# An encoder layer on one core: the rotary key's projection with high and low weight columns side by side, banks for the last halves, and other due times

## The chip, the core and the metric

The kernel runs on one of the eight cores of a Trainium2 chip. A core has five engines that run side by side and meet only at semaphores: TensorE (PE) for matmuls, with its weight loads (PEld) ahead of them, VectorE (DVE), ScalarE (ACT), GpSimd (POOL), and SyncE (SP), which here only issues DMAs. Every engine takes its own queue in order. PE writes its results to PSUM, eight banks of 128 partitions by 512 fp32 values; DVE and ACT read them from there. The metric is the device time of one execution in microseconds (us).

## What is computed

One layer of an encoder for 512 positions and a model width of 1024. Its reference, cut to what matters here:

```python
h = _rmsnorm(x, norm_mix[i])
proj = h @ w_in[i]
c_q, c_kv, k_pe, u_h = proj[..., :c1], proj[..., c1:c2], proj[..., c2:c3], proj[..., c3:]
q = (_rmsnorm(c_q, q_norm[i]) @ w_uq[i]).reshape(B, S, H, QK_HEAD_DIM)
kv = (_rmsnorm(c_kv, kv_norm[i]) @ w_ukv[i]).reshape(B, S, H, QK_NOPE_DIM + V_HEAD_DIM)
...
k = jnp.concatenate([k_nope, k_pe_h], axis=-1)
...
y_attn = _block_attention(q, k, v).reshape(B, S, MLA_WIDTH)
...
y_hyena = x0 * _bidir_long_conv(x1 * vh, h_fwd, h_bwd, hyena_bias[i])
...
x = x + y_mix @ w_out[i]
...
x = x + (jax.nn.silu(g) * u) @ w_down[i]
e = _rmsnorm(p[i] @ w_ple[i], ple_norm[i])
x = x + jax.nn.sigmoid(x @ w_ple_gate[i]) * e
```

One combined projection yields the query's latent (768 columns), the key and value latent (256), one rotary key of 32 columns (`k_pe`) that all eight heads share, and three inputs of a long convolution (512 each). Attention and convolution are normed, joined and projected; a gated MLP with a short convolution follows, and at the end an embedding (256 wide) that is projected, normed and gated by a sigmoid.

## The kernel before

Activations lie transposed: 128 channels on the partitions, 512 positions along a row. Precision comes from splitting. Each fp32 operand becomes a high part (`hi`, rounded to the matmul's input type, fp32r, by an ACT copy) and a low part (`lo`, the rest, by a DVE subtraction), and `prod3` gives three matmuls for each pair of 128-row tiles: high by high, high by low, low by high. A projection of 1024 inputs to 128 outputs is 8 x 3 = 24 matmuls of 512 columns into one PSUM bank.

PSUM is used by two tags of four banks: `mm` (`mm_ps`) and `ax` (`ax_ps`). A tile takes the bank of the tile four places before it in its tag.

Weights come in a fixed order (`stream`). `wload` loads 1024 columns by SP into one of two raw buffers (`wr`), and splits them into one of three `wh` and three `wl` buffers. From the sixth on, half of the low part is formed by an ACT copy with scale -1 and an accumulating load on POOL's queue. `ahead` keeps three weights recorded ahead of use.

Order is not written by hand. All instructions are first recorded by the class `Plan`. `cost` gives each an estimated duration, `order` gives each a due time and then lists the instructions of every engine: at each step that one which can start first, and among those within 0.02 us the one due first. A due time of a matmul is its place in PE's recorded sequence; any other instruction's is set backwards from the instructions that need its result. Nothing in this says that a bank must be empty for its next tile; a tile only gets a slot when one is free. `STRETCH`, `MARGIN` and the durations in `cost` belong to this planner. The constants at the top (`D_FILT` and the like) delay tasks that are woven into the recorded sequence by `advance`, `ENG` chooses an engine for single operations, `UQ` is the order of the six query projections, `GN` the steps of the attention at which a convolution gate is recorded, and `TAIL` the recorded order of what stands between the query projections and the attention: E and O inverse transforms, V values, G a gate, S scores, P the preparation of the second head, and R, which lets all tasks end and then forms the softmax scale from the sums of the query's squares.

Where the change touches the program:

- After the key and value latents, `in_gemm(2)` projects the rotary key. Its 32 columns are repeated four times, to 128 weight columns, so that every 32 partitions hold a copy. `rms_bcast` forms `R1`, the input norm, spread over partitions by a matmul with ones; DVE multiplies the bank by `R1`, ACT squares it (`pesq`), and `rotate` gives `kpe`.
- Between these, the loads of constants (the rotary table, the identity, selectors, four transform matrices of 512 KB) are recorded. `plan.behind = gate_consts` makes them wait for the POOL addition of the sum of x squared.
- The third and fourth weight of the stream (`w_in[2]` and `w_in[3]`) go through `wload`.
- `embedding`, recorded behind the seventh of eight output projections of the MLP, loads its input `pT`, splits it into `ph` and `pl`, and projects it in 8 x 6 matmuls.
- The last loop gates the embedding for eight tiles: a projection, a sigmoid on ACT out of the bank, a product and a sum on DVE, and the store. For the last tile this is done in two halves of 256 positions, whose matmuls write two halves of one bank. For the planner a matmul touches its whole bank.

Of the kernel before, what the change touches and what calls it, by code (L numbers as in the profile page):

```python
# [25 lines left out]
D_SIN = 2.0  # L26
D_FILT = 13.5
D_TR = 1.0
D_HALF = 8.5
D_RMS = 18.5  # L30
D_LAT = 0.0
D_UU = 13.0
D_UT = 1.0
D_MUL = 3.5
D_SPR = 6.0
D_SQ = 13.0
NTMP = 10
D_LR = 7.0
D_KC = 4.5
D_RC = 2.5  # L40
W0N = 512
# [4 lines left out]
NRH = 15  # L46
D_FT = 11.5
TAIL = 'E0 P E1 R O S0 S1 V0 V1 S2 S3 V2 G0 V3'
ENG = {'pr0': 'G', 'a53': 'V', 'a64': 'V', 'sp3': 'V', 'pr2': 'G', 'sp7': 'G', 'qa2': 'V', 'm5': 'V', 'a51': 'G', 'ah1': 'G', 'hl0': 'V', 'fwo': 'G', 'ah3': 'G', 'qa5': 'V', 'hl2': 'G', 'qa3': 'V', 'm6': 'V', 'm7': 'G', 'm2': 'V', 'qa1': 'V', 'sp5': 'G', 'xt': 'G', 'Uc': 'G', 'sp4': 'G', 'w01': 'V', 'w11': 'V', 'a61': 'G', 'pr3': 'G', 'a67': 'G', 'a63': 'V', 'u4': 'G', 'a65': 'G', 'w10': 'G', 'u3': 'G', 'sp0': 'G', 'eos': 'V', 'vx': 'A', 'vl': 'V', 'vh': 'A', 'va': 'V', 'vf': 'V', 've': 'V', 'vc': 'A', 'sx': 'A', 'sl': 'V', 'sh': 'V', 'sa': 'V', 'sf': 'V', 'se': 'V', 'sc': 'A', 'qa4': 'G', 'sp6': 'V', 'm4': 'V', 'rot2': 'G', 'cv5': 'V', 'm1': 'G', 'a62': 'V', 'rot1': 'G'}
ATT = {'pr', 'a', 'ah', 'hl', 'xt'}  # L50
PRI = {'rows': 500, 'val': 20, 'kt': 60, 'rms': -120, 'cols': 400, 'H': 0, 'gate': 150, 'uT': -120, 'io': -20, 'sq': 20, 'turn': 0, 'so': -300, 'fold': -120, 't8': 0, 'gsq': -50, 'ie': 400}
QACT = 0
UQ = [5, 2, 4, 3, 0, 1]
D_KS = 6.0
D_KR = 5.0
D_TAIL = 16.5
RFILL = 4
# [3 lines left out]
FILLS = (16, 24, 32)  # L61
GN = (4, 6, 7, 9)
CPRI = 50
EPS = 1e-6
MARGIN = 0.1
AIM = 0.0
STRETCH = {'V': 1.05, 'S': 1.05, 'G': 1.05, 'PE': 1.0, 'SP': 1.0}
NH = 8
# [154 lines left out]
class Plan:  # L223
# [50 lines left out]
    def cost(self, op):  # L274
# [11 lines left out]
        if op.eng == "PE":  # L286
            if op.fn == "transpose":
                op.dur = 0.11 if a[1].shape[0] > 8 else 0.07
            elif a[1].dtype == F32:
                op.dur = max(0.222, 0.855 * n / T) if n > 8 else 0.222  # L290
            else:
                op.dur = (n + 32) / 2400.0
            op.lat = 0.25
        elif op.eng == "V":
            if op.fn == "reduce_max":
                op.dur = 0.6
            elif op.fn in ("tensor_tensor", "stream_shuffle"):
                op.dur = 0.07 + n / 960.0
            elif op.fn == "reciprocal":
                op.dur = 0.1  # L300
            elif op.fn == "tensor_scalar" and not any(isinstance(v, View) for v in a[2:]) and not a[1].tile.tag.pool.psum:
                op.dur = 0.08 + n / 1900.0
            else:
                op.dur = 0.12 + n / 960.0
            op.lat = 0.22
            ins = [v for v in list(a[1:]) + list(kw.values()) if isinstance(v, View) and v.shape[1] * len(v.shape) > 16]
            op.port = n > 64 and len(ins) > 1 and not any(v.tile.tag.pool.psum for v in ins)
        elif op.eng == "S":
            op.dur = 0.09 + n / 1190.0
            if isinstance(kw.get("scale"), View) or isinstance(kw.get("bias"), View):  # L310
                op.dur += 0.06
            if kw.get("accum_out") is not None:
                op.dur += 0.15
            op.lat = 0.24
            op.table = TABLES.get(a[2])
        elif op.eng == "G":
            op.dur = 0.05 + (n / 780.0 if op.fn == "tensor_scalar" else n / 410.0)
            op.port = n > 64 and op.fn != "memset"
        else:
            op.dur = 0.1  # L320

    def order(self):
        clock = 5.5
        for op in self.ops:
            if op.eng == "PE":
                op.due = clock
                clock += op.dur
            else:
                op.due = None
            for p in op.preds:  # L330
                p.succs.append(op)
        for op in reversed(self.ops):
            need = clock + 50.0 if op.due is None else op.due
# [113 lines left out]
def tile_encoder_block(  # L447
# [50 lines left out]
    def wload(src, n, cut):  # L498
# [23 lines left out]
    def ahead(i):  # L522
        while len(ready) < min(i, len(stream)):
            with nullcontext():
                ready.append(wload(*stream[len(ready)]))

# [337 lines left out]
    plan.behind = None  # L864
    ckv = [xpool.tile([P, T], F32, tag="x", name="x") for _ in range(2)]
    for i in range(2):
        V.tensor_tensor(ckv[i], kv_ps[i], R1, op=ALU.mult)
    pe = tmp()
    V.tensor_tensor(pe, pe_ps, R1, op=ALU.mult)
    S.activation(pesq, pe, AF.Square)  # L870
    S.activation(pe, pe, AF.Copy, scale=pcol("gk_r"))
# [558 lines left out]

    def embedding():
# [3 lines left out]
        split(ph, pl, ptr)  # L1435
        pp = [(ph[:, i * T : (i + 1) * T], pl[:, i * T : (i + 1) * T]) for i in range(2)]
        for m in range(8):
# [16 lines left out]
    for m in range(8):  # L1454
        ps = mm_ps()
        o = 0
        for ci, nk in enumerate((8, 8, 6)):
            w = next_w()
            mms(ps, prod3(wtiles(w, nk), hid[o : o + nk]), start=ci == 0, stop=ci == 2)
            o += nk  # L1460
# [4 lines left out]
        if m == 6:  # L1465
            embedding()

    Re = const.tile([P, T], F32, tag="R1", name="Re")
    for m in range(8):
        w = next_w()  # L1470
        ps = mm_ps()
        halves = ((0, T),) if m < 7 else ((0, 256), (256, T))
        for a, b in halves:
            mms(ps[:, a:b], prod3(wtiles(w, 8), [tuple(v[:, a:b] for v in k) for k in x2]))
        if m == 0:
            rms_bcast(Re, acc7, 1024, tt4, "e")
        V.scalar_tensor_tensor(ev[m], ev[m], pcol("g_ple", m), Re, op0=ALU.mult, op1=ALU.mult)
        t = tt4()
        for a, b in halves:
            S.activation(t[:, a:b], ps[:, a:b], AF.Sigmoid)  # L1480
# [74 lines left out]
def _layout(d):  # L1555
# [99 lines left out]
```

## Time and profile before

| | us |
|---|---|
| median of 3 runs | 739.68 (739.25 to 739.82) |
| profiled execution | 739.88 |
| its span, first to last instruction | 738.1 |
| idle of PE before its first matmul | 5.68 |

The span is the part of the time in which instructions run. In the profile every instruction stands at line 441, the planner's call that issues it, so groups are told apart by tile names: `mm` and `ax` are the banks, `wh`, `wl` and `wr` the weights, `a`, `g`, `x` and `t` activations. A matmul's row gives its own time with its way through the array, about 0.39 us; in an unbroken sequence the starts lie closer together than that, and the distance of the starts is what a matmul costs. "[3.54 <-ACT t L441]" behind a row says that the engine was idle for 3.54 us before it and which instruction ended the wait. An "x2" joins two neighbours in one row.

### The profile page before, as it was taken

The page shows a single profiled execution, that of the slowest core. Times are in us where ns is not written, and L with a number is a line of the kernel's source. Part 1 is how long each engine was busy: PE and PEld are TensorE (multiplying, and loading weights), DVE is VectorE, ACT ScalarE, POOL GpSimd, SP SyncE. Part 2 cuts the span into 40 slices and gives each one's busy share as a digit, 9 for nine tenths or more (in the row PEclk, how much of TensorE's full clock was granted, in tenths as well). Part 3 has the DMA queues.
Part 4 walks back from the last instruction along what each step waited for, and adds up shares of the span by engine and source line. Part 5 has one row for each costly group of instructions (what it writes and reads, how often), then busy time and mean ns, then how long its engine had stood idle before and what let it go on. Part 6 is the DMA issues. An engine that isn't in the chain of part 4 may idle for free.

```text
span 738.1 us, 9053 instructions
## 1 busy us (share of the span) xinstructions
PE 718.2 (97%) x3254; PEld 580.8 (79%) x3254; DVE 509.6 (69%) x768; ACT 370.8 (50%) x579; POOL 177.1 (24%) x158
## 2 busy tenths in 40 slices
PE   6999999998989999999999999999999999999997
PEld 4777888875577788878888888888888888878886
DVE  6698999998689986878676676676765223242383
ACT  7564455387779985545443443434433222235331
POOL 1211101011047872422223223223322000004000
PEclk9999999999999999999999999999999999999999
DMA  7776573555352412523323223233232332333321
GB/s 246 241 187 161 124 185 86 114 122 131 75 175 59 107 44 57 133 96 89 111 87 104 97 87 113 86 97 103 86 107 81 98 114 83 96 117 106 110 104 71
DMA packets 30111, 82.83 MB, mean 112 GB/s; under 512 B 3914, under 2 KB 5258, under 8 KB 30067
## 3 DMA queue, kind: packets, MB, share of 16 engines
q1 hardware_dynamic: 24674, 72.01, 31.3%
q0 software_dynamic: 5392, 10.25, 7.4%
q8 instruction: 25, 0.41, 0.2%
q14 instruction: 20, 0.16, 0.1%
HBM read 77.00 MB, written 2.10 MB: 107 GB/s over the span
## 4 chain that ended last, share of the span: by engine, by line
PE 55%; DVE 1%; issue 0%; ACT 0%; DVEq 0%
PE mm L441 38%; PE ax L441 18%; DVE a L441 0%; DVE pl L441 0%; DVE t L441 0%; ACT t L441 0%; DVEq L1650 0%; DVE x L441 0%
## 5 line engine op out<-in xcount | busy, mean ns | idle before, releaser
L441 PE MATMUL mm<-a,wh 128*128 128x512 f32 (+1 forms) x928 | 310.4, 390 | 6.9 <-ACT wh L441 6.8
L441 ACT ACTIVATE wh<-wr 128x1024 fp32r<-128x1024 f32 (+2 forms) x117 | 119.1, 1020 | 256.3 <-PE mm L441 192.5
L441 PEld LDWEIGHTS mm<-a,wh 128*128 128x128 f32 x928 | 173.3, 189 | 45.2 <-ACT wh L441 7.6
L441 PE MATMUL mm<-a,wl 128*128 128x512 f32 (+1 forms) x464 | 171.9, 391 | 0.0
L441 DVE TENSOR_TENSOR wl<-wr,wh 128x1024 fp32r<-128x1024 f32 (+3 forms) x117 | 121.3, 1040 | 68.9 <-ACT wh L441 68.7
L441 PE MATMUL ax<-a,wh 128*128 128x512 f32 x384 | 147.1, 389 | 0.0
L441 PEld LDWEIGHTS mm<-a,wl 128*128 128x128 f32 x464 | 87.4, 189 | 19.1 <-DVE t L441 0.8
L441 DVE SCALAR_TENSOR_TENSOR f<-f,par,f 128x511 f32<-128x511 f32 x88 | 85.9, 980 | 2.7 <-ACT f L441 1.2
L441 PEld LDWEIGHTS ax<-a,wh 128*128 128x128 f32 x384 | 72.0, 188 | 14.9
L441 PE MATMUL mm<-g,wh 128*128 128x512 f32 x232 | 80.1, 397 | 3.5 <-ACT t L441 3.5
L441 PE MATMUL ax<-a,wl 128*128 128x512 f32 x192 | 74.7, 389 | 0.0
L441 PE MATMUL mm<-h,wh 128*128 128x512 f32 x192 | 65.9, 389 | 0.0
L441 POOL TENSOR_TENSOR f<-f,f 128x512 f32<-128x512 f32 x22 | 29.3, 1331 | 143.4 <-DVE f L441 125.2
L441 PEld LDWEIGHTS mm<-g,wh 128*128 128x128 f32 x232 | 43.9, 190 | 14.7 <-ACT t L441 4.0
L441 DVE TENSOR_TENSOR f<-mm,R 128x512 f32<-128x512 f32 x22 | 15.2, 691 | 46.4 <-PE mm L441 46.3
L441 POOL TENSOR_TENSOR acc<-acc,t 128x512 f32<-128x512 f32 x13 | 18.8, 1448 | 113.8 <-ACT t L441 103.1
L441 PE MATMUL mm<-g,wl 128*128 128x512 f32 x116 | 45.2, 395 | 0.0
L441 PEld LDWEIGHTS ax<-a,wl 128*128 128x128 f32 x192 | 36.0, 188 | 7.5
L441 PEld LDWEIGHTS mm<-h,wh 128*128 128x128 f32 x192 | 36.0, 188 | 7.5
L441 POOL DMA_DIRECT2D wl<-in_w_in_dram x16 | 13.9, 871 | 102.4 <-DVE wl L441 40.0
L441 ACT ACTIVATE f<-f,par 128x512 f32<-128x512 f32 x44 | 35.3, 806 | 5.2 <-DVE f L441 5.2
L441 PE MATMUL mm<-h,wl 128*128 128x512 f32 x96 | 37.4, 389 | 0.0
(242 smaller groups left out, 1007.5 us busy)
## 6 DMA issues: line engine op xcount, KB each, us to landing
wr<-in_w_up_dram SPq DMA_DIRECT2D x44, 512.0 KB, 3.5
wr<-in_w_in_dram SPq DMA_DIRECT2D x19, 512.0 KB, 3.9
wr<-in_w_down_dram SPq DMA_DIRECT2D x16, 512.0 KB, 3.5
x<-in_xT_dram SPq DMA_DIRECT2D x16, 256.0 KB, 4.4
wl<-in_w_in_dram POOLq DMA_DIRECT2D x16, 256.0 KB, 5.2
wr<-in_w_out_dram SPq DMA_DIRECT2D x8, 512.0 KB, 4.2
wr<-in_w_gate_dram SPq DMA_DIRECT2D x8, 512.0 KB, 3.5
wr<-in_w_down_dram SPq DMA_DIRECT2D x8, 384.0 KB, 3.1
```

What stands on the lines that cost most here:

```text
L441: getattr(self.handles[op.eng], op.fn)(*[real(v) for v in op.args], **{k: real(v) for k, v in op.kw.items()})
```

## The change

The rotary key's weight now has 64 distinct columns in place of 128: for each of the eight 128-row tiles, 32 columns twice. `wload_pe` loads them as 512 columns and writes the high parts into columns 0 to 63 and the low parts into columns 64 to 127 of one tile. One matmul with all 128 columns against the high part of x gives high by high on partitions 0 to 63 and low by high on 64 to 127; a second one with the 64 high columns against the low part of x adds into partitions 0 to 63. ACT copies the two halves of the bank crosswise into a temporary tile, and DVE adds bank and copy, so that each of the four groups of 32 partitions holds the whole sum. Its product with `R1` then comes from there.

`wload_halves` loads and splits `w_in[3]` in two halves by temporary tiles. The loads of constants are recorded behind the whole rotary key and wait for `pesq`. `embedding_input` loads and splits `pT` when the seventh output projection is begun. In the last loop each half of the last tile gets a bank of its own. In `order`, an instruction that touches a PSUM tile is also due before the first instruction of the tile that takes its bank, if that is recorded later. Further, `cost` has other durations for small DVE instructions, PSUM readers and ACT, and the delays, `UQ`, `GN`, `TAIL`, `ENG`, `STRETCH` and `MARGIN` have other values.

```diff
-D_FILT = 13.5
-D_TR = 1.0
-D_HALF = 8.5
-D_RMS = 18.5
+D_FILT = 13.0
+D_TR = 2.0
+D_HALF = 7.0
+D_RMS = 30.5
...
-D_SPR = 6.0
-D_SQ = 13.0
+D_SPR = 3.5
+D_SQ = 2.0
...
-TAIL = 'E0 P E1 R O S0 S1 V0 V1 S2 S3 V2 G0 V3'
+TAIL = 'R E0 E1 O P V0 S0 S1 V1 S2 G0 V2 S3 V3'
...
-UQ = [5, 2, 4, 3, 0, 1]
-D_KS = 6.0
-D_KR = 5.0
-D_TAIL = 16.5
+UQ = [5, 0, 4, 1, 2, 3]
+D_KS = 2.0
+D_KR = 7.0
+D_TAIL = 14.5
...
-GN = (4, 6, 7, 9)
+GN = [4, 6, 5, 11]
...
-MARGIN = 0.1
+MARGIN = 0.05
 AIM = 0.0
-STRETCH = {'V': 1.05, 'S': 1.05, 'G': 1.05, 'PE': 1.0, 'SP': 1.0}
+STRETCH = {'V': 1.05, 'S': 1.03, 'G': 1.05, 'PE': 1.0, 'SP': 1.0}
...
+            elif n <= 32:
+                op.dur = 0.13 if op.fn == "tensor_scalar" else 0.22
...
+            elif op.fn == "tensor_scalar":
+                op.dur = 0.3 + n / 960.0
...
-            op.dur = 0.09 + n / 1190.0
+            op.dur = max(0.14, (0.05 if a[1].tile.tag.pool.psum else 0.09) + n / 1170.0)
...
+        for pool in self.pools:
+            for tag in pool.tags.values():
+                for k, tile in enumerate(tag.tiles):
+                    tile.heir = tag.tiles[k + tag.bufs] if k + tag.bufs < len(tag.tiles) else None
         for op in reversed(self.ops):
             need = clock + 50.0 if op.due is None else op.due
             for s in op.succs:
                 need = min(need, s.due - op.dur - op.lat - AIM - (2.0 + op.byte / 2.0e5 if op.byte else 0.0))
+            for tile in {x[0] for x in op.acc}:
+                heir = tile.heir if tile.tag.pool.psum else None
+                if heir is not None and heir.first.i > op.i:
+                    need = min(need, heir.first.due - op.dur - op.lat)
             op.due = need
...
+    def wload_pe():
+        raw = tmp()
+        SP.dma_start(raw, w_in[2][:, 0:T])
+        both = wpool.tile([P, 1024], F32R, tag="wh", name="wh", bufs=3)
+        r3 = raw.rearrange("p (k c) -> p k c", k=8)
+        w3 = both.rearrange("p (k c) -> p k c", k=8)
+        S.activation(w3[:, :, 0:64], r3, AF.Copy)
+        V.tensor_tensor(w3[:, :, 64:P], r3, f32(w3[:, :, 0:64]), op=ALU.subtract)
+        return both, None
+
+    def wload_halves(src):
+        hi = wpool.tile([P, 1024], F32R, tag="wh", name="wh", bufs=3)
+        lo = wpool.tile([P, 1024], F32R, tag="wl", name="wl", bufs=3)
+        for a in (0, T):
+            raw = tmp()
+            SP.dma_start(raw, src[:, a : a + T])
+            split(hi[:, a : a + T], lo[:, a : a + T], raw)
+        return hi, lo
...
-    pe_ps = in_gemm(2)
+    pe_ps = mm_ps()
+    pe_w = next_w()[0]
+    for k in range(8):
+        both, high = (pe_ps, pe_w[:, k * P : (k + 1) * P], xs[k][0]), (pe_ps[0:64, :], pe_w[:, k * P : k * P + 64], xs[k][1])
+        for part in (both, high) if k == 0 else (high, both):
+            PE.matmul(*part, start=k == 0 and part is both, stop=k == 7 and part is both)
+        advance(T_IN / 12)
     rms_bcast(R1, accx, 1024, tmp, "x")
-    plan.behind = gate_consts
+    ckv = [xpool.tile([P, T], F32, tag="x", name="x") for _ in range(2)]
+    for i in range(2):
+        V.tensor_tensor(ckv[i], kv_ps[i], R1, op=ALU.mult)
+    pe = tmp()
+    other = tmp()
+    S.activation(other[0:64, :], pe_ps[64:P, :], AF.Copy)
+    S.activation(other[64:P, :], pe_ps[0:64, :], AF.Copy)
+    V.tensor_tensor(other, pe_ps, other, op=ALU.add)
+    V.tensor_tensor(pe, other, R1, op=ALU.mult)
+    late = S.activation(pesq, pe, AF.Square)
+    plan.behind = late
...
+        if m == 6:
+            pin = embedding_input()
...
-        ps = mm_ps()
         halves = ((0, T),) if m < 7 else ((0, 256), (256, T))
-        for a, b in halves:
+        t = tt4()
+        for i, (a, b) in enumerate(halves):
+            ps = mm_ps()
             mms(ps[:, a:b], prod3(wtiles(w, 8), [tuple(v[:, a:b] for v in k) for k in x2]))
...
```

More of the change, by code (lines that the diff above doesn't have):

```diff
@@ L26 @@
 D_SIN = 2.0
-D_FILT = 13.5
-D_TR = 1.0
-D_HALF = 8.5
-D_RMS = 18.5
+D_FILT = 13.0
+D_TR = 2.0
+D_HALF = 7.0
+D_RMS = 30.5
 D_LAT = 0.0
 D_UU = 13.0
-D_UT = 1.0
-D_MUL = 3.5
-D_SPR = 6.0
-D_SQ = 13.0
+D_UT = 0.5
+D_MUL = 3.0
+D_SPR = 3.5
+D_SQ = 2.0
 NTMP = 10
-D_LR = 7.0
-D_KC = 4.5
-D_RC = 2.5
+D_LR = 12.0
+D_KC = 6.0
+D_RC = 4.0
 W0N = 512
@@ L46 @@
 NRH = 15
-D_FT = 11.5
-TAIL = 'E0 P E1 R O S0 S1 V0 V1 S2 S3 V2 G0 V3'
-ENG = {'pr0': 'G', 'a53': 'V', 'a64': 'V', 'sp3': 'V', 'pr2': 'G', 'sp7': 'G', 'qa2': 'V', 'm5': 'V', 'a51': 'G', 'ah1': 'G', 'hl0': 'V', 'fwo': 'G', 'ah3': 'G', 'qa5': 'V', 'hl2': 'G', 'qa3': 'V', 'm6': 'V', 'm7': 'G', 'm2': 'V', 'qa1': 'V', 'sp5': 'G', 'xt': 'G', 'Uc': 'G', 'sp4': 'G', 'w01': 'V', 'w11': 'V', 'a61': 'G', 'pr3': 'G', 'a67': 'G', 'a63': 'V', 'u4': 'G', 'a65': 'G', 'w10': 'G', 'u3': 'G', 'sp0': 'G', 'eos': 'V', 'vx': 'A', 'vl': 'V', 'vh': 'A', 'va': 'V', 'vf': 'V', 've': 'V', 'vc': 'A', 'sx': 'A', 'sl': 'V', 'sh': 'V', 'sa': 'V', 'sf': 'V', 'se': 'V', 'sc': 'A', 'qa4': 'G', 'sp6': 'V', 'm4': 'V', 'rot2': 'G', 'cv5': 'V', 'm1': 'G', 'a62': 'V', 'rot1': 'G'}
+D_FT = 8.0
+TAIL = 'R E0 E1 O P V0 S0 S1 V1 S2 G0 V2 S3 V3'
+ENG = {'pr0': 'G', 'a53': 'V', 'a64': 'V', 'sp3': 'V', 'pr2': 'G', 'sp7': 'G', 'qa2': 'V', 'm5': 'V', 'a51': 'G', 'ah1': 'G', 'hl0': 'V', 'fwo': 'G', 'ah3': 'G', 'qa5': 'V', 'hl2': 'G', 'qa3': 'V', 'm6': 'V', 'm7': 'G', 'm2': 'V', 'qa1': 'V', 'sp5': 'G', 'xt': 'G', 'Uc': 'G', 'sp4': 'G', 'w01': 'V', 'w11': 'V', 'a61': 'G', 'pr3': 'G', 'a67': 'G', 'a63': 'V', 'u4': 'G', 'a65': 'G', 'w10': 'G', 'u3': 'G', 'sp0': 'G', 'eos': 'V', 'vx': 'V', 'vl': 'V', 'vh': 'A', 'va': 'A', 'vf': 'V', 've': 'A', 'vc': 'A', 'sx': 'A', 'sl': 'A', 'sh': 'A', 'sa': 'V', 'sf': 'V', 'se': 'A', 'sc': 'A', 'qa4': 'G', 'sp6': 'V', 'm4': 'V', 'rot2': 'G', 'cv5': 'V', 'm1': 'G', 'a62': 'V', 'rot1': 'G', 'ah0': 'V'}
 ATT = {'pr', 'a', 'ah', 'hl', 'xt'}
@@ L300, in cost @@
                 op.dur = 0.1
-            elif op.fn == "tensor_scalar" and not any(isinstance(v, View) for v in a[2:]) and not a[1].tile.tag.pool.psum:
+            elif n <= 32:
+                op.dur = 0.13 if op.fn == "tensor_scalar" else 0.22
+            elif op.fn == "tensor_scalar" and not a[1].tile.tag.pool.psum:
                 op.dur = 0.08 + n / 1900.0
+            elif op.fn == "tensor_scalar":
+                op.dur = 0.3 + n / 960.0
             else:
@@ L316, in cost @@
         elif op.eng == "G":
-            op.dur = 0.05 + (n / 780.0 if op.fn == "tensor_scalar" else n / 410.0)
+            op.dur = 0.05 + (n / 780.0 if op.fn == "tensor_scalar" else n / 420.0)
             op.port = n > 64 and op.fn != "memset"
@@ L524, in ahead @@
             with nullcontext():
-                ready.append(wload(*stream[len(ready)]))
+                i = len(ready)
+                ready.append(wload_pe() if i == 2 else wload_halves(w_in[3]) if i == 3 else wload(*stream[i]))
     def next_w():
@@ L864, in tile_encoder_block @@
     plan.behind = None
[L865 to L870, printed above, removed]
     S.activation(pe, pe, AF.Copy, scale=pcol("gk_r"))
@@ L1429, in tile_encoder_block, with embedding_input @@
     ev = []
-    def embedding():
+    def embedding_input():
         ptr = wpool.tile([P, 1024], F32, tag="wr", name="wr", bufs=2)
@@ L1435, in embedding @@
         split(ph, pl, ptr)
+        return ph, pl
+    def embedding(ph, pl):
         pp = [(ph[:, i * T : (i + 1) * T], pl[:, i * T : (i + 1) * T]) for i in range(2)]
@@ L1465, in tile_encoder_block @@
         if m == 6:
-            embedding()
+            embedding(*pin)
     Re = const.tile([P, T], F32, tag="R1", name="Re")
@@ L1470, in tile_encoder_block @@
         w = next_w()
-        ps = mm_ps()
         halves = ((0, T),) if m < 7 else ((0, 256), (256, T))
-        for a, b in halves:
+        t = tt4()
+        for i, (a, b) in enumerate(halves):
+            ps = mm_ps()
             mms(ps[:, a:b], prod3(wtiles(w, 8), [tuple(v[:, a:b] for v in k) for k in x2]))
[L1475 to L1479, printed above, removed]
+            if m == 0:
+                rms_bcast(Re, acc7, 1024, tt4, "e")
+            if i == 0:
+                V.scalar_tensor_tensor(ev[m], ev[m], pcol("g_ple", m), Re, op0=ALU.mult, op1=ALU.mult)
             S.activation(t[:, a:b], ps[:, a:b], AF.Sigmoid)
@@ L1588, in _layout @@
     out["w_in"] = mk(a["w_in"][0], 8, in_sel)
+    out["w_in"][2, :, 0:512] = mk(a["w_in"][0], 8, [np.tile(1024 + r(32), 2)])[0]
+    out["w_in"][2, :, 512:] = 0.0
     out["w_uq"] = mk(a["w_uq"][0], 6, uq_sel)
```

## The prediction

> **What bounds the kernel now.** First the head of the page and its busy times.
>
> ```profile
> span 738.1 us, 9053 instructions
> ...
> PE 718.2 (97%) x3254; PEld 580.8 (79%) x3254; DVE 509.6 (69%) x768; ACT 370.8 (50%) x579; POOL 177.1 (24%) x158
> ```
>
> TensorE (PE) is busy for 97% of the span, so the time is its work plus its holes. Where the holes are is told by the table of windows (columns: window, length, busy of PE, weight load, DVE, ACT, POOL with counts, granted clock, DMA share, GB/s), whose rows come from several such tables:
>
> ```profile
> 20.00:174.35 154.35, 153.97 (x668) 121.90 (x667) 140.07 (x234) 85.23 (x129) 22.09 (x28) 1.00 0.59 150
> ...
> 60.00:160.00 100.00, 100.00 (x450) 82.63 (x449) 94.48 (x160) 52.79 (x81) 12.95 (x15) 1.00 0.52 126
> 160.00:180.00 20.00, 16.46 (x68) 11.17 (x66) 18.09 (x32) 14.71 (x26) 3.45 (x4) 0.98 0.64 151
> ...
> 200.00:220.00 20.00, 18.14 (x95) 14.04 (x94) 16.23 (x43) 15.01 (x37) 6.13 (x7) 1.00 0.61 177
> 220.00:240.00 20.00, 19.21 (x119) 15.93 (x118) 19.55 (x52) 19.79 (x42) 15.69 (x18) 1.00 0.27 65
> ...
> 178.28:182.32 4.04, 4.04 (x13) 2.85 (x14) 3.23 (x7) 3.98 (x10) 0.00 (x1) 0.62 0.78 191
> ```
>
> PE is full from 20 on but for 0.38 us, until a hole near 175 with a slow clock behind it; more holes lie in the attention from 200 on, where DVE and ACT are nearly full too. The waits of PE give the causes (total, times, longest):
>
> ```profile
> PE mm L441 <- ACT wh L441: 6.8, 2, 5.7
> PE mm L441 <- ACT t L441: 3.5, 1, 3.5
> PE ax L441 <- DVE ptl L441: 1.5, 1, 1.5
> PE ax L441 <- DVE pl L441: 1.0, 1, 1.0
> PE ax L441 <- DVE st L441: 0.8, 2, 0.4
> PE mm L441 <- ACT pth L441: 0.5, 2, 0.3
> PE ax L441 <- ACT pr L441: 0.5, 1, 0.5
> ```
>
> Of the 6.8 us, 5.7 are the first inputs' way, and the change leaves these loads as they are. The other rows are what it can reach. Where there is no hole, a matmul costs its start-to-start step; the chain that ended last has one long unbroken piece of 512-column matmuls:
>
> ```profile
> 564.28 97.06 PE mm L441 x428
> ```
>
> 97.06 / 428 = 0.227 us each.
>
> **The change part by part.** *Rotary key, 24 matmuls to 16.* Eight fewer: 8 x 0.227 = 1.82 us. They stand on the path, because PE is full there. Eight of the sixteen have 64 weight columns instead of 128. No row shows that shape; the nearest has 8 columns:
>
> ```profile
> 194.93 0.62 PE L441 MATMUL ax<-t,sel 128*8 128x512 f32 x2
> ...
> 178.64 0.57 ACT L441 ACTIVATE t<-ax 8x512 f32<-8x512 f32 x1
> ...
> L441 DVE TENSOR_TENSOR t<-mm,R x21: 669/681/692, 29.3 to 300.0; 128x512 f32<-128x512 f32 x21
> ```
>
> Two take 0.62 with the last one's own 0.40 in it, a step of 0.22 to 0.23: few columns are no cheaper and no dearer. Bounds for the eight: 0 and 1.8; I take no saving. The merge of the two halves adds two ACT copies from PSUM (0.57 each by the 8-row one) and one DVE addition (0.68 by the bank readers). Set against them, this weight is split at half width, so one saves about the other. What waits for the result is the rotary part of the keys, which meets the other parts only after the query projections, and PE's bank comes free without the norm that its reader waits for today. I cost it at nothing; if the cover were gone, it would be 2 x 0.57 + 0.68 = 1.8, all of the gain. The two half loads of the next weight go into temporary tiles and split in halves, at two more fixed parts of an instruction, hidden likewise.
>
> *PSUM readers due with their bank.* The new rule makes an instruction that reads a bank due before the first write of the tile that takes the bank next. The case for it is the second hole:
>
> ```profile
> 174.35 0.39 PE L441 MATMUL mm<-g,wl 128*128 128x512 f32 x1
> 178.28 0.73 PE L441 MATMUL mm<-g,wh 128*128 128x512 f32 x2 [3.54 <-ACT t L441]
> ...
> 172.34 0.62 ACT L441 ACTIVATE t<-accy 128x512 fp32r<-128x512 f32 x1
> 174.55 1.06 ACT L441 ACTIVATE wh<-wr 128x1024 fp32r<-128x1024 f32 x1 [1.59 <-PE mm L441]
> ...
> 177.55 0.67 ACT L441 ACTIVATE t<-mm,par 128x512 f32<-128x512 f32 x1
> ```
>
> PE waits for the bank of a finished query projection. Its copy (t<-mm,par) stands in ACT's queue behind a weight split that waits 1.59 us for a buffer, and behind four more instructions. Ahead of the split, in those idle 1.59 us, the copy would have been done before PE asks at 174.58. So the whole hole goes: 178.28 - 174.35 - 0.227 = 3.70 us. What is late next is the weight split, by one copy of 0.67; it is of the value weights, which come into use behind the query projections. Behind the hole the clock falls: in the window from 178.28 its mean is 0.62, so 0.38 x 4.04 = 1.5 us are lost, which go with the hole.
>
> The same rule acts on the attention's banks:
>
> ```profile
> 215.30 0.75 DVE L441 SCALAR_TENSOR_TENSOR a<-x,par,a 128x512 fp32r<-128x512 f32 x1 [0.64 <-ACT a L441]
> ...
> 216.30 0.68 DVE L441 TENSOR_TENSOR ptl<-ax,pth 128x512 fp32r<-128x512 f32 x1
> ...
> 217.13 0.63 PE L441 MATMUL ax<-ident,a 128*128 128x128 f32 x4 [1.51 <-DVE ptl L441]
> ```
>
> DVE does a low half for a later GEMM before the split that empties the bank. Bounds: 0 (DVE is 19.55 of 20 busy just behind, so a hole filled here may open there) and 1.5. I take the middle, 0.75.
>
> *Embedding's input sooner.*
>
> ```profile
> 656.00 0.33 SPq L441 DMA_DIRECT2D wr<-in_pT_dram  x1
> ...
> 661.36 0.69 DVE L441 TENSOR_TENSOR x<-x,mm 128x512 f32<-128x512 f32 x1 [1.94 <-PE mm L441]
> ...
> 661.96 1.22 DVE L441 TENSOR_TENSOR pl<-wr,ph 128x1024 fp32r<-128x1024 f32 x1
> ...
> 663.24 0.50 PE L441 MATMUL ax<-pl,wh 128*128 128x512 f32 x1 [1.01 <-DVE pl L441]
> ```
>
> The low half is split only behind the bank's reader at 661.36. Recorded one projection earlier (66 matmuls, 15 us), load and split are done long before. The 1.0 us goes; the weights behind it on SP are later by one 0.33 issue and one buffer, under a stage in which DVE and ACT are mostly idle.
>
> *Banks for the last halves.*
>
> ```profile
> 733.38 0.66 ACT L441 ACTIVATE t<-mm 128x256 f32<-128x256 f32 x2 [1.32 <-PE mm L441]
> 733.80 0.76 DVE L441 TENSOR_TENSOR t<-t,f 128x256 f32<-128x256 f32 x2 [0.29 <-ACT t L441]
> 734.48 0.75 DVE L441 TENSOR_TENSOR t<-t,x 128x256 f32<-128x256 f32 x2
> ```
>
> Both halves' gates, products and sums follow the last matmul, to 735.23. With a bank of its own the first half is out earlier, and one of each remains: the second product starts 0.76 / 2 behind 733.80 and takes about 0.4, to 734.56. Gain 0.7 us.
>
> *Constants behind the key's square.* Two DMA issues on SP and six with a memset on POOL move from a wait for a POOL addition to one for ACT's square near 30. The first weights gain what these transfers took from them, which can't be more than the 0.38 us that PE lacks in 20 to 174; behind the moved ones stand weight loads on both queues, and the price of that, up to 2 us, is worked out in the rivals. I take 0, since the weights are recorded three ahead.
>
> *New costs, delays and lists.* They add and remove no instruction, and shift the order by fractions of a microsecond in the stages that PE fills. Bounds: the other waits of the attention above gone, or a bare chain; both are rivals, and I take 0.
>
> Sum: 1.8 + 3.7 + 1.5 + 0.75 + 1.0 + 0.7 = 9.45. The profiled execution took 739.88 (span 738.1, 1.8 around it), 0.2 over the median of 739.68; from the median, **730.2 us**.
>
> **The rivals.** *The hole only moves (0.18).* ACT is busy for 14.7 of 20 us in 160 to 180, and DVE for 94% over 60 to 160; if the readers come late because these engines are late, and not because of their order, some or all of the hole returns. For it: the rows above show ACT without a pause from 174.55 on. Against: it paused 1.59 just before. Half the hole back, without the clock (the 1.51-us hole at 217 left the clock at 1.00 in its row): 730.2 + 1.85 = 732; all of it back with the clock: 735.4, and without the attention's gain 736.2.
>
> *The clock's share is not regular (0.05).* The profiled execution lost 1.5 to the clock; if the others did not, the gain is that much smaller: 731.7. The three runs of before span 0.57 us (739.25 to 739.82), which speaks for one loss in all of them. [...]
>
> *The attention gives more (0.12).* All 1.5 of the hole at 217, and up to the 0.8, 0.5 and 0.5 of the last three waits above: 730.2 - 0.75 - 1.8 = 727.7.
>
> *The constants get in the way (0.06).* Their loads now wait for an ACT instruction near 30, and the accumulating weight loads queue behind them on POOL:
>
> ```profile
> 21.52 0.58 POOL L441 DMA_DIRECT2D dft<-in_c_dft_dram  x1
> 35.94 0.90 POOL L441 DMA_DIRECT2D wl<-in_w_in_dram  x1 [13.84 <-DVE t L441]
> ...
> 29.99 0.63 ACT L441 ACTIVATE qr<-t 128x512 f32<-128x512 f32 x1 [2.65 <-DVE t L441]
> ...
> L441 PE MATMUL ax<-g,qs x24: 389/389/389, 75.2 to 114.9; 128*128 128x512 f32 x24
> ```
>
> Six issues at 0.58 to 0.90 are 3.5 to 5.4 us from 30 on, to 33.5 to 35.4, where the first accumulating load stands today. A constant itself is not needed before 75. If that load slips by 2, PE waits up to 2: 732.
>
> *Slower: the scale chain stands in PE's queue (0.05).* The list of the tail now begins with R, which ends the tasks and forms the softmax scale; before it stood behind both even inverses and prep. PE takes its queue in order. If the turns of this chain come ahead of the inverses and values that fill PE today, PE waits at each hop.
>
> ```profile
> 185.77 1.02 PE L441 MATMUL ax<-accx,ones 128*8 128x512 f32 x2
> ...
> 203.91 0.19 DVE L441 SCALAR_TENSOR_TENSOR sT<-sT,qs 128x32 f32<-128x32 f32 x1
> ```
>
> The chain runs for 18.3 us, all filled today. Bare by more than the 9.45 gained, it ends slower; bare for 15, 745. Against it: the order is made from ready times, so a fill goes first as long as these are about right.
>
> **Chances.** Forecast (728.5 to 732) 0.52; the hole moves 0.18, the clock 0.05, the attention 0.12, the constants 0.06, slower 0.05; 0.02 for gains that cancel. Faster by over 0.2% (1.5 us, about what a measurement here can tell) holds nearly all but the last two: 0.90; same 0.04, slower 0.06, the slower rival and a little of the hole's with more than one hole. Range 727 to 736.5: it takes in the forecast and the rivals but the slower one, and leaves out some 0.12.
>
> **What would show it.** Eight matmuls fewer into the key's bank, and PE's count at 3246; no PE wait on ACT t near 170 and the granted clock 1.00 from 160 to 200; no wait on pl; one sigmoid behind the last matmul; PE's waits in 200 to 280 no longer. It is wrong if a hole of over 1 us stands at another place of 160 to 280, or if PE waits near 40.

## The result, and the profile after

The changed kernel takes 727.53 us (median of 4 runs, 726.46 to 728.12) where the kernel before took 739.55 (739.25 to 739.82) on the same chip: a ratio of 0.9828, 95% interval 0.9811 to 0.9845, so 12 us less by the medians and 12.7 by the ratio. The forecast was 730.2. Scaled to the 739.68 from which it started, the result is 726.96, just under the lower end of the range (727). The direction was right, the reasons only in part, and the gain was a quarter to a third larger than the 9.45 us of the forecast. One execution among all that follow was slow (808.34 us, of the rotary key alone with a tile elsewhere), and its ratio leaves it out.

The head and the busy times of the page after:

```profile
span 726.3 us, 9038 instructions
...
PE 713.0 (98%) x3246; PEld 578.6 (80%) x3246; DVE 504.5 (69%) x766; ACT 377.9 (52%) x588; POOL 178.9 (25%) x158
```

The eight matmuls are gone (3254 to 3246). The waits of PE after (total, times, longest):

```profile
PE mm L453 <- ACT wh L453: 6.8, 2, 6.3
PE mm L453 <- DVE a L453: 0.9, 1, 0.9
PE ax L453 <- DVE st L453: 0.7, 1, 0.7
PE ax L453 <- ACT pr L453: 0.4, 1, 0.4
PE mm L453 <- ACT pth L453: 0.2, 1, 0.2
```

The waits on `t`, `ptl` and `pl` of before have left the list, and there is a new one, on `a`. By stage, from the first matmul on `ckh` (the high part of the key and value latent, with which the up-projection begins) to the first score and from there to the last turn (columns as before), first of the kernel before, then of the changed one:

```profile
148.92:206.70 57.78, 54.24 (x222) 36.74 (x221) 47.22 (x89) 43.19 (x83) 7.03 (x9) 0.97 0.51 115
206.70:277.72 71.02, 67.70 (x406) 55.71 (x405) 65.51 (x165) 64.69 (x139) 49.92 (x53) 1.00 0.32 91
```

```profile
147.02:196.40 49.38, 49.38 (x216) 34.76 (x215) 44.33 (x85) 40.70 (x79) 6.92 (x8) 1.00 0.52 115
196.40:267.71 71.31, 69.61 (x415) 57.36 (x414) 67.58 (x168) 66.20 (x144) 50.05 (x55) 1.00 0.37 102
```

The first stage is 8.4 us shorter: PE has no hole in it and the clock never falls. ACT's order there after:

```profile
168.44 0.67 ACT L453 ACTIVATE t<-mm,par 128x512 f32<-128x512 f32 x1
170.38 0.85 ACT L453 ACTIVATE wh<-wr 128x768 fp32r<-128x768 f32 x1 [1.27 <-PE mm L453]
171.13 0.58 ACT L453 ACTIVATE accy<-mm 128x512 f32<-128x512 f32 x1
...
180.09 1.05 ACT L453 ACTIVATE wh<-wr 128x1024 fp32r<-128x1024 f32 x1
```

The copy that empties the first query projection's bank (168.44) now stands ahead of the split of the value weights (the one with 1024 columns, 180.09), as the prediction wanted, and even ahead of the last query weight's (170.38). Whether the bank rule put it there is what the experiments asked.

To compare stages in which the number of matmuls differs, the tables below give what PE lost in a stretch: its length less the steps of its matmuls (0.227 us for 512 columns and less in proportion, 0.11 to 0.12 for 256, about 0.47 for the full-precision ones with `ones` and `x`, 0.085 for a transposition, 0.32 for a selector, all read from unbroken pieces). A wrong step would shift both columns alike, so the differences are what counts. A turn is the transposition of one block of 128 by 512 attention weights, four matmuls with the identity; there are 32. Of the profiled executions, in us:

| stretch | before | after |
|---|---|---|
| first matmul to the first `ident,pq` matmul of the mixer (some 93) | 5.5 | 5.0 |
| first `ckh` matmul to first score | 8.7 | 1.6 |
| first score to ninth turn | 5.5 | 4.0 |
| ninth to last turn | 6.7 | 6.5 |
| last turn to the MLP's norm | 0.5 | 1.2 |
| first `ph` matmul to the embedding's norm | 1.3 | 0.0 |

The span fell by 11.8: 1.8 for eight matmuls, 0.5 in the first stretch, 7.0 behind `ckh`, 1.6 in the attention, 1.3 at the embedding, 0.8 behind the last matmul; 0.6 were given back by a later first matmul (6.30, before 5.68; in the 18 profiles of this document it starts anywhere between 5.55 and 7.14) and 0.7 in the output projection.

### The profile page after: what moved, and what is told of

It is laid out like the page before. It is cut to its first block, busy times and chain, and to the rows that moved or that the text cites. A ratio compares the mean times of both kernels' runs of the same rounds, so it can differ in the third digit from the quotient of the medians.

```text
span 726.3 us, 9038 instructions
## 1 busy us (share of the span) xinstructions
PE 713.0 (98%) x3246; PEld 578.6 (80%) x3246; DVE 504.5 (69%) x766; ACT 377.9 (52%) x588; POOL 178.9 (25%) x158
## 4 chain that ended last, share of the span: by engine, by line
PE 90%; ACT 4%; DVE 3%; issue 1%; DMA 1%; POOL 1%; SPq 0%; ACTq 0%; POOLq 0%; DVEq 0%
PE mm L453 64%; PE ax L453 26%; ACT pr L453 1%; DVE st L453 1%; DMA wr<-in_w_in_dram 1%; ACT pth L453 1%; DVE ptl L453 1%; ACT a L453 0%; DVE t L453 0%; ACT t L453 0%; POOL pr L453 0%; ACT ks L453 0%; DVE a L453 0%; SPq L453 0%; DVE x L453 0%
## 5 line engine op out<-in xcount | busy, mean ns | idle before, releaser
L453 PE MATMUL mm<-a,wh 128*128 128x512 f32 (+2 forms) x928 | 310.2, 391 | 7.7 <-ACT wh L453 6.8
L453 ACT ACTIVATE wh<-wr 128x1024 fp32r<-128x1024 f32 (+2 forms) x115 | 116.6, 1016 | 188.1 <-PE mm L453 178.6
L453 PEld LDWEIGHTS mm<-a,wh 128*128 128x128 f32 (+1 forms) x928 | 173.8, 189 | 45.2 <-ACT wh L453 7.5
L453 PE MATMUL mm<-a,wl 128*128 128x512 f32 (+1 forms) x456 | 168.1, 391 | 0.0
L453 DVE TENSOR_TENSOR wl<-wr,wh 128x1024 fp32r<-128x1024 f32 (+3 forms) x115 | 119.4, 1041 | 66.9 <-ACT wh L453 66.8
L453 PE MATMUL mm<-g,wh 128*128 128x512 f32 x232 | 78.0, 392 | 0.0
L453 ACT ACTIVATE f<-f 128x512 f32<-128x512 f32 x22 | 13.9, 632 | 56.1 <-DVE f L453 56.1
```

Of the source, the lines that this page charges most:

```text
L453: getattr(self.handles[op.eng], op.fn)(*[real(v) for v in op.args], **{k: real(v) for k, v in op.kw.items()})
```

## Experiments: one part alone

**The bank rule alone**, the kernel before with

```diff
+            for tile in {x[0] for x in op.acc}:
+                heir = tile.heir if tile.tag.pool.psum else None
+                if heir is not None and heir.first.i > op.i:
+                    need = min(need, heir.first.due - op.dur - op.lat)
```

> The kernel before with nothing but the bank rule in the planner. If the hole behind 174.35 is a fault of order (theory), PE's wait on ACT t is gone or under 0.5 us, the granted clock is 1.00 from 160 to 200, and the time is 733.5 to 735 (739.6 less 5.2, or less 5.2 and up to 0.75 in the attention). If the new delays, lists and costs are what closes it (rival), PE still waits over 2 us for an ACT copy in 165 to 185, and the time is within 2 us of 739.6.

Measured: 740.74, ratio 1.0016 (1.0007 to 1.0025). The waits of PE:

```profile
PE mm L449 <- DVE a L449: 2.2, 1, 2.2
PE mm L449 <- ACT t L449: 1.5, 1, 1.5
```

The hole behind the up-projection is halved (3.5 to 1.5) and its slow clock gone, but a hole of 2.2 opens in the output projection at 295 us, with 3.41 us of half clock behind it (mean granted clock 0.997 over the span). The rule alone brings nothing. ACT's queue shows why half the hole stays:

```profile
173.87 1.06 ACT L449 ACTIVATE wh<-wr 128x1024 fp32r<-128x1024 f32 x1 [1.59 <-PE mm L449]
174.83 0.67 ACT L449 ACTIVATE t<-mm,par 128x512 f32<-128x512 f32 x1
```

The rule took the copy past the four other instructions, but not past the split, which waits the same 1.59 us as before.

**The new delays, lists, engine choices and durations alone** (called the new figures below):

```diff
...
-D_SQ = 13.0
+D_SQ = 2.0
...
-UQ = [5, 2, 4, 3, 0, 1]
...
-D_TAIL = 16.5
+UQ = [5, 0, 4, 1, 2, 3]
...
+D_TAIL = 14.5
...
```

> The kernel before with only the new delays, lists, engine choices and planner durations. Theory (moves only): within 3 us of 739.6, the wait on ACT t still above 2 us. Rival: the hole closes by these alone, 733 to 736, wait on ACT t under 0.5 us.

Measured: 741.31, ratio 1.0015 (0.9999 to 1.0031). The same hole is nearly closed (`ACT t` 0.6), without the rule: the copy (177.91) now stands ahead of the split of the value weights (178.65); others open at 49 to 67 us and at 209 (`DVE x` 2.5).

**The rotary key alone** (`wload_pe`, `wload_halves`, 16 matmuls, merge; the constants at their old place):

> The kernel before with only the rotary key in 16 matmuls (its weight's load and split, the half loads of the next weight, the crosswise merge); constants still behind the sum of x squared. Theory: eight matmuls at 0.227 us are gone from a full PE, the key stage ends 1.8 us sooner and, with the hole unchanged, the time is 737.2 to 738.2. Rival (DVE and ACT take it back, or the hole grows by it): 739 to 740, the wait on ACT t longer by 1.5 to 1.8 us.

Measured: 751.46, ratio 1.0160 (1.0145 to 1.0175), 12 us slower where 2 less were due. PE's waits show one of 8.7 us on `pth`, which the prediction had not named. It is followed up below.

**The embedding's input and the halves' banks alone:**

```diff
+        if m == 6:
+            pin = embedding_input()
...
-        ps = mm_ps()
...
-        for a, b in halves:
...
+        for i, (a, b) in enumerate(halves):
+            ps = mm_ps()
...
```

> The kernel before with only the embedding's input one projection earlier and a bank for each last half. Theory: the wait on pl (1.0 us by the waits, about 1.2 from start to start) is gone and the stretch from the last matmul to the end is 0.7 us shorter: 737.5 to 738. Rival (the weights behind the earlier load are late, or a store of the first half delays the second): the one or the other is under 0.3, time 738.5 to 739.6.

Measured: 737.81, ratio 0.9978 (0.9969 to 0.9987). These two do what they say, 1.6 us.

## Experiments: all but one part

**Without the bank rule:**

> The changed kernel without the bank rule, all else kept. Theory: a wait of PE on ACT t or on another reader of a bank comes back in 150 to 200 with 2 to 5 us in all, and the attention's waits grow by 0.5 to 1.5; time 730 to 734. Rival (delays, lists and costs do it): no wait over 1 us there, time within 1.5 us of 727.5.

Measured: 741.35, ratio 1.0027 (1.0014 to 1.0040). The stretch behind `ckh` loses 1.5 us, as little as with the rule, but PE waits 8.2 us for `pth` at 207.

**With the old figures** (delays, lists, engine choices and durations):

> The changed kernel with the delays, lists, engine choices and planner durations of before; the rotary key, the bank rule, the embedding and the halves as changed. Of the 12 us gained, 9.45 were worked out from these four. Theory: the rest of 2 to 3 us is the new delays and lists, so the time is 729 to 731. Rival (the four were undersized and the lists do nothing): within 1 us of 727.5. Other rival (structure and lists only work together): over 733, with a hole of over 2 us in 30 to 280.

Measured: 752.44, ratio 1.0178 (1.0163 to 1.0193). Again 8.1 us on `pth`, and holes of 1.5 to 2.2 at 52, 178 and 309 us.

**With the constants at their old place:**

```diff
-    plan.behind = late
+    plan.behind = gate_consts
```

> The changed kernel with the loads of constants waiting again for the sum of x squared. Theory (the move costs and brings nothing): within 1 us of 727.5, the first 100 us as in the changed kernel to 0.7 us. Rival: the early constants take bandwidth from the first weights and PE waits 1 to 2 us more on weights in the first 40 us, time 728.5 to 729.5.

Measured: 727.04, ratio 0.9841 (0.9819 to 0.9863), not to be told from the changed kernel. Moving the constants costs and brings nothing that shows.

**With the rotary key in 24 matmuls** (and, as before, the constants early):

> The changed kernel with the rotary key in 24 matmuls, loaded, merged and gated as before. Theory: slower by 1.8 us, 729.3 (728.8 to 730.3). Rival (the delays are set for 16 matmuls, so the order falls apart): over 731, with a new wait of PE of over 1 us in 20 to 280.

Measured: 733.49, ratio 0.9916 (0.9895 to 0.9936), 6 us more than with 16, not 1.8: it has new waits on `wl` (0.9) at 50 us and `a` (1.4) at 209, and 3.4 us of half clock.

So the parts don't add. Before one can say what a part is worth, the 8-us hole of three of these runs has to go.

## Experiments: where a tile lies

In the run with the rotary key alone, SyncE's DMA issues around the attention's start, SyncE's waits there, ScalarE's row and PE's wait:

```profile
198.41 1.16 SPq L441 DMA_DIRECT2D qr<-g  x2
210.17 1.10 SPq L441 DMA_DIRECT2D kr<-x  x2
...
214.71 1.12 SPq L441 DMA_DIRECT2D kr<-x  x2
```

```profile
SPq L441 <- PE ax L441: 10.9, 1, 10.9
```

```profile
221.54 0.63 ACT L441 ACTIVATE ks<-kr 96x512 fp32r<-96x512 f32 x1 [8.27 <-DMA kr<-x]
```

```profile
PE mm L441 <- ACT pth L441: 8.7, 1, 8.7
```

Read backwards: PE waits for `pth`, an ACT copy; ACT stands 8.27 us before `ks<-kr`, which waits for the raw key's load; SyncE issued that load at 214.71, late behind another `kr` (210.17, of head 2), for which it had waited 10.9 us on PE. That `kr` copies a tile that PE does not write. But it lies in memory that the closed pool `ft` held before, and a tile's place is given out in the order in which tiles are first touched. From the built programs (bytes per partition):

```
                     kr of head 2      over                 last read by
before               216992 to 219040  uu0, pq0             transforms, early
changed              216992 to 219040  uu2                  transforms, early
rotary alone         216992 to 219040  ckl1                 value matmuls
without bank rule    216992 to 219040  ckl1                 value matmuls
old delays           216992 to 219040  ckl1                 value matmuls
```

`ckl1` is a low part of the key and value latent; the last matmul that reads it starts at 209.74 us in the run above, and SyncE goes on at 210.17 (the row of the wait names a neighbour of that matmul on PE). The three kernels with the hole are those where `kr` lies over it. A test that changes the place and leaves the order of every engine's instructions as it is (the two built programs differ in addresses and in waits alone):

```diff
-                raw = pool.tile([P, T], F32, tag=f"{nm}r", name=f"{nm}r")[0:96, :]
+                raw = (at if nm + pool.name == "qap" else pool).tile([P, T], F32, tag=f"{nm}r", name=f"{nm}r")[0:96, :]
```

> Same order of instructions on every engine as the run with the rotary key alone (751.46 us). Only the place in SBUF differs: the raw query of the heads with a pool of their own lies in the pool ahead, so that the raw key of head 2 (kr) moves up by 2 KB and lies over the input's tile uu1, last read early, and no longer over ckl1, last read by the value matmuls. Theory (placement): SyncE's wait on PE before kr (10.9 us in that run) and the 8.7 us hole in the attention's start are gone, and with them the 10.6 us that the stretch from the first score to the eighth turn lost over the kernel before: 736 to 741 us, near the kernel before less the 1.8 us of the eight matmuls (737.7). Rival (order): the list's order of the work causes the hole, and the time stays at 751 +- 1.

Measured: 741.92, ratio 1.0023 (1.0009 to 1.0036), 9.5 us less than the same order at the old place, and a little over the expected band (the kernel before took 740.03 beside it). SyncE's issues and PE's first waits:

```profile
198.67 1.16 SPq L441 DMA_DIRECT2D qr<-g  x2
199.87 1.23 SPq L441 DMA_DIRECT2D kr<-x  x2
...
204.54 1.12 SPq L441 DMA_DIRECT2D kr<-x  x2
```

```profile
PE mm L441 <- ACT wh L441: 6.4, 1, 6.4
PE mm L441 <- ACT t L441: 3.5, 1, 3.5
PE ax L441 <- DVE st L441: 2.8, 5, 1.3
```

`kr` follows `qr` at once, and the wait for `pth` is down to 0.3. The stretch from the first score to the ninth turn loses 5.45, to the hundredth what the kernel before loses.

The same edit in the other two kernels:

> The changed kernel without the bank rule (741.35 us), with the same order of instructions on every engine and the raw key of head 2 at another place. Theory (placement): the hole before the value side's first weighing (8.2 us, and 10 us of half clock behind it) is gone, 12.4 us less in the stretch from the first score to the eighth turn: 728 to 731 us; the bank rule would then be worth 1 to 3 us of the change and not the whole. Rival (order, so the bank rule itself): 741 +- 1.

Measured: 732.84, ratio 0.9889 (0.9866 to 0.9913): 8.5 us less, but 2 above the expected band.

> The changed kernel with the old delays and cost model (752.44 us), same order of instructions, raw key of head 2 at another place. Theory (placement): 10.6 us less, 739 to 743 us; the holes at 51, 178 and 309 us stay, since they have nothing to do with the place. Rival (order): 752 +- 1.

Measured: 741.36, ratio 1.0022 (1.0006 to 1.0038): 11 us less, within the band.

And the other way round: the changed kernel with the key put over a late tile (the edit above, and `ab` of "k" moved to `at` likewise), again with each engine's order as it was.

> The changed kernel (727.5 us), same order of instructions on every engine; the raw query and the split key of the heads' second pool lie in the pool ahead, so that the raw key of head 2 lies over ckl0, last read by the value matmuls at about 203 us, and not over uu2. Theory (placement): SyncE waits some 9 us for PE before this transfer (issued at 193.4 us without the wait), the next key's transfer (197.1 us) goes to about 206.5 us, ScalarE stands before its ks for some 6 us, and matmuls wait for pth: 731 to 739 us. Rival (order): 727.5 +- 1.

Measured: 737.22, ratio 0.9952 (0.9936 to 0.9968): 9.7 us slower than the changed kernel, by place alone. SyncE's issues in the changed kernel, then here, and ScalarE and PE here:

```profile
192.14 1.18 SPq L453 DMA_DIRECT2D qr<-g  x2
193.36 1.23 SPq L453 DMA_DIRECT2D kr<-x  x2
...
197.07 1.12 SPq L453 DMA_DIRECT2D kr<-x  x2
```

```profile
192.37 1.17 SPq L453 DMA_DIRECT2D qr<-g  x2
203.83 1.11 SPq L453 DMA_DIRECT2D kr<-x  x2
...
207.43 1.11 SPq L453 DMA_DIRECT2D kr<-x  x2
```

```profile
214.15 0.63 ACT L453 ACTIVATE ks<-kr 96x512 fp32r<-96x512 f32 x1 [7.43 <-DMA kr<-x]
```

```profile
PE mm L453 <- ACT pth L453: 7.8, 1, 7.8
```

Same chain, same size. By the ratios to the kernel before, which ran beside each, place is worth 9 to 12 us in all four pairs. The kernel before and the changed one both lie on the good side, so it is no part of the 12 us.

## Experiments: what the rest is made of

With the place mended the parts can be compared (ratio to the kernel before; a single part without the others, a pair of parts and all three with the embedding and the halves, which are worth 0.9978; "delays" stands for all new figures). In none of these runs does PE wait for `pth` longer than 0.4 us at a time, so none has the hole of the last section:

| | ratio |
|---|---|
| rule / delays / rotary key alone | 1.0016 / 1.0015 / 1.0023 |
| rule and rotary key | 1.0022 |
| rule and delays | 0.9916 |
| delays and rotary key | 0.9889 |
| all three | 0.9828 |

The new figures of the planner are in every row that gains. Taken out of the changed kernel they cost 14 us (1.0022 less 0.9828), the rotary key 6.5, the rule 4.5; each of the three put alone into the kernel before brings nothing. By stretch, what PE lost with the place mended:

| stretch | before | after | no rule | old figures |
|---|---|---|---|---|
| start | 5.5 | 5.0 | 4.8 | 7.9 |
| `ckh` to first score | 8.7 | 1.6 | 1.5 | 5.2 |
| first score to ninth turn | 5.5 | 4.0 | 7.7 | 4.8 |
| ninth to last turn | 6.7 | 6.5 | 10.3 | 8.3 |
| last turn to the MLP's norm | 0.5 | 1.2 | 0.1 | 4.7 |

So the rule earns nothing behind the up-projection once the figures are new; in these executions (6.1 us apart, where the ratios say 4.5) it earns 7.4 us in the attention and costs 1.1 in the output projection. Against the kernel before, though, the attention gains 1.6 only: without the rule the changed kernel loses 5.8 more there than the kernel before (the new figures alone lose 3.2), and the rule takes these back. Without it PE's largest waits in the attention are

```profile
PE ax L445 <- ACT pr L445: 2.2, 4, 1.1
PE mm L445 <- DVE x L445: 1.9, 1, 1.9
```

and 3.41 us of half clock follow the second (mean granted clock 0.998 over the span). The rule also leaves 1.5 of the hole behind the up-projection where the figures are old (5.2 in the last column). Which of the figures close it:

**Old delays and lists, new durations:**

> The changed kernel with the old delays and orders of tasks, but the new durations of the planner, with the raw key of head 2 off the tile ckl1 as in the run that had delays and durations both old (741.36 us). Theory (the delays close the holes): the time stays near that run's, 739 to 743 us. Rival (the planner's durations do it): 727 to 731 us.

Measured: 742.63, ratio 1.0044 (1.0026 to 1.0062), in the band of the theory; PE's wait of 1.5 us on `t` is there again.

**New delays and lists, old durations:**

> The changed kernel with the planner's old durations and the new delays; the raw key of head 2 lies off the late tiles by itself. Theory (the delays): 727 to 731 us, the stretch from the first matmul on ckh to the first score loses under 2 us. Rival (the durations): 738 to 742 us.

Measured: 731.93, ratio 0.9893 (0.9877 to 0.9910), a little over the band. With the old delays and lists the whole gain is gone, with the old durations alone some 5 us of it, spread over five stretches at 0.3 to 1.2 each.

**Only the query side's delays old:**

```diff
-D_RMS = 30.5
+D_RMS = 18.5
...
-D_SQ = 2.0
+D_SQ = 13.0
...
-UQ = [5, 0, 4, 1, 2, 3]
-D_KS = 2.0
-D_KR = 7.0
-D_TAIL = 14.5
+UQ = [5, 2, 4, 3, 0, 1]
+D_KS = 6.0
+D_KR = 5.0
+D_TAIL = 16.5
```

> The changed kernel with the old delays and order of the query side alone (D_SQ, D_TAIL, D_KS, D_KR, D_RMS, UQ); the other delays, the durations and the bank rule stay, and the raw key of head 2 is off the late tiles. Theory (the query side's delays, with the bank rule, close the hole behind the up-projection): the stretch from the first matmul on ckh to the first score loses 5 us again, as with all old delays (5.2), and 1.6 in the changed kernel: 731 to 735 us. Rival (the other side's delays, of filters and mixer): 727 to 729 us.

Measured: 731.57, ratio 0.9888 (0.9872 to 0.9904). The time is in the band, its place is not: the stretch behind `ckh` loses 3.1, 1.5 more than after and not the 3.6 more of all old figures, and the profile shows no wait of PE in it; 2.5 more are lost between the first score and the ninth turn. So the hole stays closed when the query side's delays are old, with the copy (171.09) ahead of the split of the value weights (174.38), and the theory is refuted; the rival's 727 to 729 isn't met either.

**The rule only ahead of the last fills of the output projection.** The hole that the rule opens there, in the changed kernel, on VectorE, GpSimd and PE:

```profile
280.71 0.68 DVE L453 TENSOR_TENSOR t<-mm,R 128x512 f32<-128x512 f32 x1
281.31 0.68 DVE L453 TENSOR_TENSOR yp<-yp,Ra 128x512 f32<-128x512 f32 x1
281.91 1.96 DVE L453 SCALAR_TENSOR_TENSOR a<-yp,par,a 128x512 fp32r<-128x512 f32 x1
```

```profile
281.73 1.58 POOL L453 TENSOR_TENSOR x<-x,t 128x512 f32<-128x512 f32 x1
```

```profile
283.92 0.50 PE L453 MATMUL mm<-a,wh 128*128 128x512 f32 x1 [0.87 <-DVE a L453]
```

```diff
-                if heir is not None and heir.first.i > op.i:
+                if heir is not None and heir.first.i > op.i and op.i < self.rule_to:
...
+    plan.rule_to = len(plan.ops)
     while fill < 8:
```

> The changed kernel (727.5 us) with the bank rule only for what stands ahead of the last fills of the output projection. Theory (collision): in the changed kernel the rule puts the product t<-mm,R at 280.71 us between the products with Ra, GpSimd's x<-x,t follows it at 281.73 and runs for 1.58 us, and VectorE's a<-yp,par,a beside it takes 1.96 us where one takes 0.74 us; that makes the hole of 0.87 us at 283.92 us. Without the rule there GpSimd's sum comes later, a<-yp,par,a takes 0.74 us, the hole goes: 726.0 to 727.0 us. Rival (VectorE is just busy, or the bank's reader is then late for the next matmul): 727.5 us or more.

VectorE then:

```profile
280.68 1.90 DVE L453 TENSOR_TENSOR yp<-yp,Ra 128x512 f32<-128x512 f32 x3
282.49 1.41 DVE L453 SCALAR_TENSOR_TENSOR a<-yp,par,a 128x512 fp32r<-128x512 f32 x2
```

No sum on GpSimd stands beside it, two low halves take 1.41 where one took 1.96, PE's wait on `a` is 0.3 in place of 0.9, and the stretch loses 0.6 in place of 1.2. So the collision makes this hole, as the theory has it. The gain in time isn't shown: 727.86, ratio 0.9829 (0.9814 to 0.9844). The profiled execution lost 1.25 us more in its first 95 us than the changed kernel's, with the same order there, and that start differs between executions by more than the gain. No version tried is measurably faster than the changed kernel.

## Why the prediction was right and wrong

- *Eight matmuls, 1.82*: right. They are gone, and the eight with 64 columns are no cheaper:

```profile
L453 PE MATMUL mm<-a,wh 128*64 128x512 f32 x8 | 3.0, 393 | 0.0
```

  The mean of 393 ns is that of 128 columns (391). The merge is hidden, as taken: the run with the new key alone loses 3.9 us in the first stretch, with the tile elsewhere 4.1, the kernel before 5.5. But on time the eight matmuls show only together with the new figures (6.5 us by their removal, nothing alone).
- *The hole behind the up-projection, 3.70, and its clock, 1.5, go by the bank rule*: the hole and its clock went, but not by the rule. The step "ahead of the split, in those idle 1.59 us, the copy would have been done" is what the rule does not do: alone it leaves the copy behind the split, with 1.5 us of the hole, and without the rule the hole is closed too. The new delays and lists took the copy ahead of the split of the value weights, in every run that has them. The stretch gained 7.0, not 5.2. Of this the clock is 1.7, not 1.5: its slow stretch is 3.41 us long and reaches beyond the window of the prediction's row.
- *"New costs, delays and lists ... I take 0"* is the step that failed. Taken out with the place mended, they cost 14 us, and they close the hole that the sum gave to the bank rule. The reason given, that they shift the order by fractions of a microsecond in stages that PE fills, doesn't hold: one copy behind a split instead of ahead of it left a hole of 1.5 us, and behind four more instructions one of 3.5 us with half clock after it. That a sum with 5.2 of its 9.45 us under the wrong cause came within 3 us of the result was in part luck. The named bound, the attention's other waits gone, was also too narrow, since the old figures lose in every stretch.
- *Attention, 0.75 of 1.5*: mis-sized; 1.6, and this is where the rule works, though mostly against losses that come with the other parts (7.4 us by its removal). The rival that gave it all 1.5 was nearer.
- *Embedding 1.0, halves 0.7*: right, 1.3 and 0.8 in the profiles, 1.6 us in the run of both alone. The run with the rotary key alone, however, has no wait on `pl` either.
- *Constants, 0*: right as far as the run that puts them back can tell.
- *The hole only moves*: not in the changed kernel, but so it went in the run of the rule alone (1.5 left, 2.2 elsewhere). The 0.9 at 284 has the same cause as that 2.2.
- *Slower, the scale chain bare*: didn't come. A slower case as dear did lie near, by a way that the prediction didn't name: a tile's place.

What stays open: which single delay or list takes the copy ahead of the split, how the new figures act in the other stretches, and whether the 12 us would survive another small edit, which may again move `kr` over a late tile.

## What to carry to other kernels

When a planner makes the order, don't cost the parts of a change one by one, as if they added up: run each part alone and each left out, and look in every one for a hole where the part does nothing. If a DMA stands still for an engine that gives it no data, look at what lay in its memory before; move the tile with the order fixed, which is a clean test. An instruction that comes earlier on one engine sends its successor off sooner on another, and what runs beside that one may take longer: here 1.96 us in place of 0.74.

## What the runs showed of the hardware

*Place in SBUF.* The same instructions in the same order took 751.5 or 741.9, and 727.5 or 737.2, by the addresses of a few tiles; SyncE's wait points to one of them, the 2-KB `kr` of head 2.

*VectorE beside GpSimd.* A low half that takes 0.74 us took 1.96 while GpSimd's sum ran; in the run of the rule alone two of them, beside two such sums, took 4.27:

```profile
293.43 4.27 DVE L449 SCALAR_TENSOR_TENSOR a<-yp,par,a 128x512 fp32r<-128x512 f32 x2 [0.29 <-ACT a L449]
```

```profile
293.70 2.78 POOL L449 TENSOR_TENSOR x<-x,t 128x512 f32<-128x512 f32 x2
```

In the changed kernel 281.91 to 283.87 is the rest of GpSimd's sum (to 283.31) and 0.56 more, where one low half alone takes 0.74; and 4.27 is the 2.78 of two sums and 1.49, twice 0.74. What makes VectorE slower there the runs don't show.

*The clock.* The windows of the run with the old query delays:

```profile
207.42:210.83 3.41, 1.60 (x7) 0.90 (x7) 3.37 (x9) 3.41 (x8) 2.03 (x3) 1.00 0.43 162
210.83:214.24 3.41, 3.25 (x14) 3.06 (x14) 2.36 (x7) 3.41 (x9) 3.41 (x4) 0.50 0.50 112
```

PE's longest hole there is 1.12 us, but three together leave PE busy for 1.60 of 3.41, and the next window runs at half clock. In the run with the rotary key in 24 matmuls PE was busy for 1.85 of the 3.41 us from 210.30 on, and from 213.71 to 217.13 the clock was 0.50. In the kernel before, though, PE was busy for 1.55 of the 3.41 us from 215.00 on, and the clock stayed at 1.00 up to 227. So PE's busy share in such a stretch doesn't alone tell whether half clock follows, and what else does isn't shown.

The loss behind the hole of 3.54 in the kernel before:

```profile
175.84:179.25 3.41, 0.97 (x4) 0.84 (x5) 2.75 (x6) 3.41 (x8) 0.86 (x1) 1.00 0.53 87
179.25:182.66 3.41, 3.41 (x11) 2.34 (x11) 2.45 (x5) 3.35 (x8) 0.00 (x0) 0.50 0.79 190
182.66:186.07 3.41, 3.41 (x15) 2.35 (x14) 3.26 (x7) 1.73 (x3) 0.00 (x0) 1.00 0.00 0
```

PE was busy for 0.97 of 3.41 us, the next 3.41 ran at half clock, and those behind them at 1.00 again. Over the span the mean granted clock was 0.996 in this execution and 0.994 to 0.998 in all 70 of the kernel before that ran beside the experiments; in the four of the changed kernel it was 0.999 or 1.00.
